# One-hot weight rows of the expert stage: one 256-column VectorE operation per token replaced by two of 128 columns

## The chip, the cores and the metric

The kernel runs on one core of one Trainium2 chip. The core has five engines with queues of their own: TensorE (PE; its weight loads are listed apart as PEld), VectorE (DVE), ScalarE (ACT), GpSimd (POOL) and SyncE (SP, which here only issues transfers). The metric is the device time of one execution in microseconds (us), as the median of several runs. Beside it there is one profiled execution with a trace of every instruction; its span runs from the first to the last instruction.

## What is computed

A transformer-like block (feed-forward, two kinds of attention, feed-forward) is followed by a second block with a long convolution, a gated recurrence and, at its end, a layer of 16,384 single-neuron experts. The change lies in that last layer, which the reference writes so:

```
s = jnp.einsum('blhpd,hpkd->blhpk', q, keys).astype(jnp.float32)
ts, ti = lax.top_k(s, K)
cand = ts[..., 0, :, None] + ts[..., 1, None, :]
cs, ci = lax.top_k(cand.reshape(B, L, PEER_HEADS, K * K), K)
e1 = jnp.take_along_axis(ti[..., 0, :], ci // K, axis=-1)
e2 = jnp.take_along_axis(ti[..., 1, :], ci % K, axis=-1)
experts = e1 * N_KEYS + e2
g = jax.nn.softmax(cs, axis=-1).astype(x.dtype)
...
act = jax.nn.gelu(jnp.einsum('td,tkd->tk', xt, u_tab[et])) * gt
return jnp.einsum('tk,tkd->td', act, v_tab[et])
```

There are 256 tokens. Each has 8 heads with 16 chosen experts, so 128 slots, and each slot has two indices (e1 and e2, both below 128) and a weight g.

## The kernel before

Nothing is gathered: the kernel works on all 16,384 experts for all tokens. Let an expert be the pair (e1, e2). A dense table of weights `gd` of shape [e1, e2, token] holds for each token its 128 weights at the chosen pairs and zero elsewhere. The products of the tokens with the first expert table (`us`) go through gelu to `st`, are multiplied by `gd` later, and then meet the second table (`vs`).

All large products are made in three TensorE passes over a high and a low part of each operand (`mm3`, L303 to L305). The weights come as tiles of 128 x 1024 numbers. A class `Stream` loads them on SP's queue (`raw`), lets ScalarE round them to the high part (`wh`, L247), and lets VectorE subtract to get the low part (`wl`, L249); it keeps four tiles ahead of TensorE.

In the stage of the change, from 1110 to 1387 us of the trace, TensorE runs down the first table. One call of `experts_in` (L1414) takes two table tiles of 128 experts; each tile is 8 x 3 matmuls of 256 columns. In between, a generator `weights_dense` (L1536) builds `gd` token by token; `paced` (L1575) calls it about three times for each table tile, so that it is through four tiles before the table ends. One step of the generator does this:

- for every fourth token, one VectorE operation (L1546) makes the one-hot rows of e1 of four tokens, 128 x 512 (tile `oh1`, printed as `oh`);
- for each token, VectorE makes the row of e2 (L1551, the changed line): per slot, 128 columns that hold the high part of g where the column is e2 and zero elsewhere, and 128 more with the low part. The tile is `oh2`, printed as `oh`; `iota` holds 0 to 127 in each partition, `eT` the indices and weights with the slots on partitions, `wp` the high and the low part of the weights;
- for the token four steps back (LAG), TensorE multiplies the two (L1561, 128 x 256 into PSUM), and for each pair of tokens ScalarE copies the low half to `gd` (L1566) and VectorE adds the high half (L1567).

The order on each engine is the order in which the program is written. VectorE's queue in this stage thus holds only four kinds of work: `wl` L249, the one-hot rows L1546 and L1551, and the sum L1567. The tile `oh2` has six buffers.

Of the kernel before, what the change touches and what calls it, by code (L numbers as in the profile page):

```python
# [10 lines left out]
F32 = mybir.dt.float32  # L11
# [5 lines left out]
ALU = mybir.AluOpType  # L17
# [265 lines left out]
def body(ctx, tc, a, o, upto=99):  # L283
    nc = tc.nc
# [6 lines left out]
    def psum(tag):  # L291
        return PS.tile([128, 512], F32, tag=tag, name=tag, bufs={"mm": 2, "acc": 3, "od": 1, "tr": 2}[tag])

    def accs():
        return [psum("acc"), psum("acc"), psum("acc"), psum("od")]
# [37 lines left out]
    def gemm_rows(acc, w, xh, xl, start, stop):  # L333
        h, lo = w
        for tt in range(2):
            ts_ = slice(tt * 128, tt * 128 + 128)
            for hf in range(2):
                cs = slice(hf * 512, hf * 512 + 512)
                mm3(acc[2 * tt + hf], xh[:, ts_], xl[:, ts_], h[:, cs], lo[:, cs], start, stop)

    def split(h, lo, src, eng=None):
        nc.scalar.copy(h, src)  # L342
        (eng or nc.vector).tensor_tensor(lo, src, h.bitcast(F32), op=ALU.subtract)  # L343
# [58 lines left out]
    def finish(acc, ops):  # L402

        for n, i in ((0, 0), (0, 1), (1, 0), (1, 1), (0, 2), (0, 3), (1, 2), (1, 3)):
            (h, lo), xh, xl = ops[n]
            ts_, cs = slice(i // 2 * 128, i // 2 * 128 + 128), slice(i % 2 * 512, i % 2 * 512 + 512)
            mm3(acc[i], xh[:, ts_], xl[:, ts_], h[:, cs], lo[:, cs], False, n == 1)
# [260 lines left out]
    with tc.tile_pool(name="mix", bufs=1) as MP:  # L668
# [300 lines left out]
        for b in range(4):  # L969
# [3 lines left out]
            for j in range(2):  # L973
# [4 lines left out]
                                           op0=ALU.add, op1=ALU.mult)  # L978
# [431 lines left out]
    iota = PP.tile([128, 128], F32, name="iota")  # L1410
    eT = [PP.tile([128, 3, 128], F32, name=f"eT{tt}") for tt in range(2)]
    stored = [DP.tile([128, 8 if i < 15 else 4, T], F32, name=f"act{i}") for i in range(16)]

    def experts_in(i, between=pump.step):  # L1414
        pt = psum("mm")
        gemm_w(pt[:, :T], ws.next(), xs_x)
        between()
        gemm_w(pt[:, T:], ws.next(), xs_x)
        st = PP.tile([128, 2, T], F32, tag="st", name="st", bufs=2)
        last[i] = st  # L1420
        nc.scalar.activation(st, pt.rearrange("p (e t) -> p e t", e=2), AF.Gelu_apprx_tanh)  # L1421
        if i < 62:
            nc.scalar.dma_start(stored[i // 4][:, 2 * (i % 4):2 * (i % 4) + 2, :], st)
# [107 lines left out]
    with tc.tile_pool(name="dense", bufs=1) as GP:  # L1531
        gd = GP.tile([128, 128, T], F32, name="gd")

        wp = GP.tile([128, 2, 128], F32R, name="wp")

        def weights_dense():  # L1536

            o1s, ohs = {}, {}
            for t in range(T + LAG):
                if t < T:  # L1540
                    tt, tl = divmod(t, 128)
                    if tl == 0:
                        split(wp[:, 0], wp[:, 1], eT[tt][:, 2])
                    if t % ONE == 0:
                        o1 = GP.tile([128, ONE, 128], F32R, tag="oh1", name="oh1", bufs=2)
                        nc.vector.tensor_tensor(o1, iota[:, None, :].to_broadcast([128, ONE, 128]),  # L1546
                                                eT[tt][:, 0, tl:tl + ONE, None].to_broadcast([128, ONE, 128]),
                                                op=ALU.is_equal)
                        o1s[t // ONE] = o1
                    oh = GP.tile([128, 2, 128], F32R, tag="ow", name="oh2", bufs=6)  # L1550
                    nc.vector.scalar_tensor_tensor(oh, iota[:, None, :].to_broadcast([128, 2, 128]),  # L1551
                                                   eT[tt][:, 1, tl:tl + 1],
                                                   wp[:, :, tl:tl + 1].bitcast(F32).to_broadcast([128, 2, 128]),
                                                   op0=ALU.is_equal, op1=ALU.mult)
                    ohs[t] = oh
                u = t - LAG
                if u >= 0:
                    if u % 2 == 0:
                        pt = psum("acc")
                    oh = ohs.pop(u)  # L1560
                    nc.tensor.matmul(pt[:, u % 2 * T:u % 2 * T + T], o1s[u // ONE][:, u % ONE],  # L1561
                                     oh.rearrange("p n e -> p (n e)"), start=True, stop=True)
                    if u % 2 == 1:
                        v = pt.rearrange("p (t n e) -> p n e t", t=2, n=2)
                        g = gd[:, :, u - 1:u + 1]
                        nc.scalar.copy(g, v[:, 1])  # L1566
                        nc.vector.tensor_tensor(g, v[:, 0], g, op=ALU.add)  # L1567
                yield

        pump.add(weights_dense())  # L1570
        left = 128 - 2 * n_in[0]
        total = T + LAG
        busy = left - 4

        def paced(i):  # L1575
            for _ in range(min(i + 1, busy) * total // busy - min(i, busy) * total // busy):
                pump.step()

        sv = {}

        def fetch(b):
            if b < 16:
                sv[b] = P0.tile([128, 8, T], F32, tag="lT" if b % 2 else "hT", name="sv")
                nc.gpsimd.dma_start(sv[b][:, :8 if b < 15 else 4, :], stored[b])

        order = list(range(124, 128)) + list(range(124))

        def act_split(n):
            e = order[n]
            src = last[e // 2] if e >= 124 else sv[e // 8][:, e % 8 - e % 2:e % 8 - e % 2 + 2, :]  # L1590
            if e % 2 == 0:
                nc.vector.tensor_tensor(src, src, gd[:, e:e + 2, :], op=ALU.mult)  # L1592
            ah = GP.tile([128, T], F32R, tag="ow", name="ah", bufs=6)
            al = GP.tile([128, T], F32R, tag="ow", name="al", bufs=6)
            split(ah, al, src[:, e % 2])
            if e % 8 == 7 and e < 120:
                fetch(e // 8 + 2)
            return ah, al

        for i in range(left // 2):  # L1600
            experts_in(n_in[0] + i, lambda: paced(2 * i))
            paced(2 * i + 1)
            if i == left // 2 - 2:
                pump.drain()
                ws.pool_every = 0
                nxt = [act_split(0), act_split(1)]
        fetch(0)
        fetch(1)
        acc = accs()
        for n in range(126):  # L1610
            nxt.append(act_split(n + 2))
            ah, al = nxt.pop(0)
            gemm_rows(acc, ws.next(), ah, al, n == 0, False)
        gf = P0.tile([128, D], F32, tag="raw", name="gf", bufs=RAW)
        nc.scalar.dma_start(gf, a["gains"][FINAL:FINAL + 1, :].to_broadcast([128, D]))
        x2 = [P0.tile([128, D], F32, tag="raw", name="x2", bufs=RAW) for tt in range(2)]
        for tt in range(2):
            nc.scalar.dma_start(x2[tt], res[tt * 128:(tt + 1) * 128, :])
        finish(acc, [(ws.next(), *nxt[n]) for n in range(2)])
        jk = P0.tile([128, 1024], F32, tag="wh", name="jk", bufs=NH)  # L1620
        ys = [P0.tile([128, D], F32, tag="wl", name="ys", bufs=NL) for tt in range(2)]
        rs = [None, None]

        def scaled(tt, hf):
            y = ys[tt][:, HALVES[hf]]
            if hf:
                nc.scalar.activation(y, y, AF.Copy, scale=rs[tt])
            else:
                nc.vector.tensor_scalar(y, y, rs[tt], None, op0=ALU.mult)
            (nc.scalar if tt and hf else nc.sync).dma_start(o[tt * 128:tt * 128 + 128, HALVES[hf]], y)  # L1630

        for tt in range(2):
            fn = RowNorm(GP, lambda hf: x2[tt][:, HALVES[hf]], jk[:, :512])
            for hf, sl in enumerate(HALVES):
                nc.vector.tensor_tensor(x2[tt][:, sl], acc[2 * tt + hf], x2[tt][:, sl], op=ALU.add)
                fn.half(hf)
            if tt:
                scaled(0, 0)
                scaled(0, 1)
            for sl in HALVES:  # L1640
                nc.vector.tensor_tensor(ys[tt][:, sl], x2[tt][:, sl], gf[:, sl], op=ALU.mult)
            rs[tt] = fn.root()
        for hf in range(2):
            scaled(1, hf)
# [19 lines left out]
```

## Time and profile before

| what | value |
|---|---|
| median of 3 runs | 1755.02 us |
| lowest, highest | 1753.38, 1756.79 us |
| the profiled execution | 1756.68 us |
| its span | 1754.9 us |
| PE busy over the span | 98% |
| DVE busy over the span | 74% |
| ACT busy over the span | 53% |

Busy shares over the whole span mix many stages. A matmul's record reaches over the start of the next one, and so does a VectorE operation's; the distance from start to start is what a queue of such operations costs.

### The profile page before, as it was taken

How to read it: one execution, taken by the hardware profiler on the slowest of the kernel's cores; microseconds unless marked ns; L12 is line 12 of the kernel's file. 1: busy time of each engine (PE TensorE's matmuls, PEld its weight loads, DVE VectorE, ACT ScalarE, POOL GpSimd, SP SyncE). 2: the span in 40 equal slices, each digit the busy share in tenths (PEclk: the TensorE clock that was granted, in tenths of full speed). 3: DMA queues.
4: the chain of work that ended last, by engine and by line, in shares of the span. 5: the costliest groups of instructions: out<-in, count | busy, mean ns of one | idle time of the engine just before them, and what ended most of it. 6: DMA issues, size and time to landing. Idle time of an engine off the chain costs nothing.

```text
span 1754.9 us, 30439 instructions
## 1 busy us (share of the span) xinstructions
PE 1719.0 (98%) x11794; PEld 1573.9 (90%) x11794; DVE 1307.4 (74%) x2237; ACT 931.7 (53%) x1524; POOL 151.3 (9%) x151
## 2 busy tenths in 40 slices
PE   8999999999999999999999999999999999999998
PEld 7999899999899987998899999999999988888886
DVE  5665678846765654788777999999999876766775
ACT  5544556654465444778444455555555544555544
POOL 3000100000100111000004634000000000000000
PEclk9999999999999999999899999999999999999999
DMA  7646464444466553453166567666665677776674
GB/s 231 201 160 201 144 192 145 135 154 134 145 215 199 187 164 129 158 192 121 60 193 204 175 223 225 217 193 198 195 199 190 216 253 236 255 243 239 238 246 166
DMA packets 93410, 332.08 MB, mean 189 GB/s; under 512 B 10552, under 2 KB 10707, under 8 KB 90960
## 3 DMA queue, kind: packets, MB, share of 16 engines
q1 hardware_dynamic: 79488, 287.73, 51.0%
q0 software_dynamic: 3696, 21.67, 3.5%
q10 hardware_dynamic: 10080, 20.71, 3.3%
q8 instruction: 93, 1.52, 0.4%
q14 instruction: 53, 0.43, 0.1%
HBM read 311.73 MB, written 18.35 MB: 188 GB/s over the span
## 4 chain that ended last, share of the span: by engine, by line
PE 79%; DVE 15%; issue 3%; ACT 1%; DMA 1%; POOL 1%; POOLq 0%; SPq 0%; ACTq 0%; DVEq 0%
PE mm L303 14%; PE mm L305 14%; PE mm L304 14%; PE acc L305 8%; PE acc L303 8%; PE acc L304 8%; DVE oh L1551 5%; DVE wl L249 3%; PE od L303 2%; PE od L304 2%; PE od L305 2%; DVE gd L1567 2%; DVE oh L1546 2%; PE tr L1305 1%; PE acc L719 1%
## 5 line engine op out<-in xcount | busy, mean ns | idle before, releaser
L249 DVE TENSOR_TENSOR wl<-raw,wh 128x1024 fp32r<-128x1024 f32 x508 | 620.9, 1226 | 281.5 <-ACT wh L247 279.7
L303 PE MATMUL mm<-hT,wh 128*128 128x256 f32 (+1 forms) x2496 | 711.4, 285 | 0.4 <-ACT qb L1462 0.4
L304 PE MATMUL mm<-lT,wh 128*128 128x256 f32 (+1 forms) x2496 | 703.3, 282 | 0.0
L305 PE MATMUL mm<-hT,wl 128*128 128x256 f32 (+1 forms) x2496 | 702.9, 282 | 0.0
L247 ACT CAST wh<-raw 128x1024 fp32r<-128x1024 f32 x544 | 570.2, 1052 | 181.3 <-PE mm L304 71.8
L303 PEld LDWEIGHTS mm<-hT,wh 128*128 128x128 f32 x2496 | 471.9, 189 | 8.3 <-issue 4.3
L304 PEld LDWEIGHTS mm<-lT,wh 128*128 128x128 f32 x2496 | 470.4, 188 | 3.4 <-issue 1.4
L305 PEld LDWEIGHTS mm<-hT,wl 128*128 128x128 f32 x2496 | 472.2, 189 | 0.0
L303 PE MATMUL acc<-wh,ah 128*128 128x512 f32 x516 | 202.0, 391 | 0.0
L305 PE MATMUL acc<-wh,al 128*128 128x512 f32 x516 | 201.8, 391 | 0.0
L304 PE MATMUL acc<-wl,ah 128*128 128x512 f32 x516 | 201.4, 390 | 0.0
L342 ACT CAST ah<-sv 128x256 fp32r<-128x256 f32 x124 | 50.5, 407 | 156.7 <-DVE sv L1592 126.6
L1551 DVE SCALAR_TENSOR_TENSOR oh<-iota,eT,wp 128x256 fp32r<-128x256 f32 x256 | 116.1, 483 | 0.0
L305 PEld LDWEIGHTS acc<-wh,al 128*128 128x128 f32 x516 | 96.9, 188 | 20.9
L304 PEld LDWEIGHTS acc<-wl,ah 128*128 128x128 f32 x516 | 97.0, 188 | 19.4 <-issue 0.2
L303 PEld LDWEIGHTS acc<-wh,ah 128*128 128x128 f32 x516 | 96.9, 188 | 19.4 <-issue 0.3
L249 POOL TENSOR_TENSOR wl<-raw,wh 128x1024 fp32r<-128x1024 f32 x36 | 86.1, 2406 | 58.4 <-ACT wh L247 58.4
L1421 ACT ACTIVATE st<-mm 128x512 f32<-128x512 f32 x64 | 38.4, 600 | 96.5 <-PE mm L305 96.2
L343 DVE TENSOR_TENSOR al<-sv,ah 128x256 fp32r<-128x256 f32 x124 | 52.5, 423 | 35.1 <-ACT ah L342 35.0
L1566 ACT COPY gd<-acc 128x256 f32<-128x256 f32 x128 | 46.6, 402 | 58.8 <-PE acc L1561 42.2
L303 PE MATMUL od<-wh,ah 128*128 128x512 f32 x172 | 67.3, 391 | 0.0
L304 PE MATMUL od<-wl,ah 128*128 128x512 f32 x172 | 67.2, 390 | 0.0
(390 smaller groups left out, 2053.6 us busy)
## 6 DMA issues: line engine op xcount, KB each, us to landing
raw<-in_ws_dram SPq DMA_DIRECT2D x288, 512.0 KB, 3.7
raw<-in_us_dram SPq DMA_DIRECT2D x128, 512.0 KB, 3.6
raw<-in_vs_dram SPq DMA_DIRECT2D x128, 512.0 KB, 4.2
act<-st ACTq DMA_DIRECT2D x62, 256.0 KB, 2.7
sv<-act POOLq DMA_DIRECT2D x15, 1024.0 KB, 7.2
gate_w<-in_gate_w_dram ACTq DMA_DIRECT2D x2, 1024.0 KB, 5.8
gain<-in_gains_dram POOLq DMA_DIRECT2D x3, 512.0 KB, 7.1
res<-x SPq DMA_DIRECT2D x2, 512.0 KB, 4.5
```

The lines of the kernel that those rows point to most:

```text
L247: nc.scalar.copy(h, raw)
L249: eng.tensor_tensor(lo, raw, h.bitcast(F32), op=ALU.subtract)
L303: nc.tensor.matmul(out, lh, rh, start=start, stop=False)
L304: nc.tensor.matmul(out, lh, rl, start=False, stop=False)
L305: nc.tensor.matmul(out, ll, rh, start=False, stop=stop)
L342: nc.scalar.copy(h, src)
L343: (eng or nc.vector).tensor_tensor(lo, src, h.bitcast(F32), op=ALU.subtract)
L1421: nc.scalar.activation(st, pt.rearrange("p (e t) -> p e t", e=2), AF.Gelu_apprx_tanh)
L1546: nc.vector.tensor_tensor(o1, iota[:, None, :].to_broadcast([128, ONE, 128]), eT[tt][:, 0, tl:tl + ONE, None].to_broadcast([128, ONE, 128] ...
L1551: nc.vector.scalar_tensor_tensor(oh, iota[:, None, :].to_broadcast([128, 2, 128]), eT[tt][:, 1, tl:tl + 1], wp[:, :, tl:tl + 1].bitcast(F3 ...
L1566: nc.scalar.copy(g, v[:, 1])
L1567: nc.vector.tensor_tensor(g, v[:, 0], g, op=ALU.add)
```

## The change

The changed line makes the row of one token. Before, one operation with two tensor inputs covered both halves: `iota`, read twice, is compared with the token's e2 (one number per partition, read from `eT`), and multiplied by a second tensor input, the two columns of `wp` spread over 128 columns each. After, each half is an operation of its own with one tensor input (`iota`) and two numbers per partition, e2 from `eT` and the weight from `wp`.

```diff
                     oh = GP.tile([128, 2, 128], F32R, tag="ow", name="oh2", bufs=6)
-                    nc.vector.scalar_tensor_tensor(oh, iota[:, None, :].to_broadcast([128, 2, 128]),
-                                                   eT[tt][:, 1, tl:tl + 1],
-                                                   wp[:, :, tl:tl + 1].bitcast(F32).to_broadcast([128, 2, 128]),
-                                                   op0=ALU.is_equal, op1=ALU.mult)
+                    for j in range(2):
+                        nc.vector.tensor_scalar(oh[:, j], iota, eT[tt][:, 1, tl:tl + 1],
+                                                wp[:, j, tl:tl + 1].bitcast(F32), op0=ALU.is_equal, op1=ALU.mult)
```

On VectorE, in the middle of the stage, stood these rows for parts of three table tiles (`oh` with a 128x512 shape is the one-hot of four tokens, with 128x256 the changed row):

```order
L1546 TENSOR_TENSOR oh_13658<-iota,eT_9964 128x512
L1551 SCALAR_TENSOR_TENSOR oh_13660<-iota,eT_9964,wp 128x256
L1551 SCALAR_TENSOR_TENSOR oh_13664<-iota,eT_9964,wp 128x256
L1567 TENSOR_TENSOR gd<-acc,gd 128x128x2
L1551 SCALAR_TENSOR_TENSOR oh_13669<-iota,eT_9964,wp 128x256
L249 TENSOR_TENSOR wl<-raw,wh 128x1024
```

At the same place there stand now:

```order
L1546 TENSOR_TENSOR oh_13750<-iota,eT_9964 128x512
L1552 TENSOR_SCALAR oh_13752<-iota,eT_9964,wp 128x128 x2
L1552 TENSOR_SCALAR oh_13757<-iota,eT_9964,wp 128x128 x2
L1566 TENSOR_TENSOR gd<-acc,gd 128x128x2
L1552 TENSOR_SCALAR oh_13763<-iota,eT_9964,wp 128x128 x2
L249 TENSOR_TENSOR wl<-raw,wh 128x1024
```

Each of the 256 rows of L1551 has become two, in the same place, and nothing else has moved; the lines behind the change count one less. On TensorE, ScalarE, GpSimd and SyncE no row differs but for these line numbers.

## Rows read from the trace of the kernel before

**Rows 1.** The page's part 1, busy time of the engines.

```profile
PE 1719.0 (98%) x11794; PEld 1573.9 (90%) x11794; DVE 1307.4 (74%) x2237; ACT 931.7 (53%) x1524; POOL 151.3 (9%) x151
```

**Rows 2.** Windows: length, busy us of PE, PEld, DVE, ACT, POOL; PEclk; DMA.

```profile
1110.00:1200.00 90.00, 88.69 (x738) 87.44 (x737) 90.00 (x172) 47.85 (x82) 0.00 (x0) 1.00 0.62 199
1200.00:1300.00 100.00, 97.56 (x804) 95.58 (x803) 99.99 (x194) 53.08 (x91) 0.00 (x0) 1.00 0.61 194
1300.00:1387.00 87.00, 85.24 (x705) 83.78 (x704) 87.00 (x167) 46.28 (x80) 0.00 (x0) 1.00 0.61 197
1387.00:1400.00 13.00, 13.00 (x106) 12.68 (x104) 8.76 (x11) 6.85 (x12) 1.09 (x2) 1.00 0.65 208
1400.00:1755.00 355.00, 346.51 (x1529) 286.69 (x1527) 243.53 (x323) 174.47 (x261) 10.46 (x20) 1.00 0.69 236
```

**Rows 3.** Waits of TensorE, 1110 to 1387 us: total, times, longest.

```profile
PE acc L1561 <- DVE oh L1551: 3.5, 13, 0.5
```

**Rows 4.** Groups of instructions by line, 1110 to 1387 us: busy us, mean ns.

```profile
L303 PE MATMUL mm<-hT,wh 128*128 128x256 f32 x662 | 185.5, 280 | 0.0
...
L1551 DVE SCALAR_TENSOR_TENSOR oh<-iota,eT,wp 128x256 fp32r<-128x256 f32 x256 | 116.1, 483 | 0.0
L249 DVE TENSOR_TENSOR wl<-raw,wh 128x1024 fp32r<-128x1024 f32 x83 | 101.3, 1221 | 0.0
L1567 DVE TENSOR_TENSOR gd<-acc,gd 128x256 f32<-128x256 f32 x126 | 55.5, 440 | 0.0
...
L1546 DVE TENSOR_TENSOR oh<-iota,eT 128x512 fp32r<-128x512 f32 x64 | 43.9, 687 | 0.0
```

**Rows 5.** Timeline of VectorE in the middle of the stage: start us, us.

```profile
1182.08 1.21 DVE L249 TENSOR_TENSOR wl<-raw,wh 128x1024 fp32r<-128x1024 f32 x1
1183.21 0.68 DVE L1546 TENSOR_TENSOR oh<-iota,eT 128x512 fp32r<-128x512 f32 x1
1183.81 0.87 DVE L1551 SCALAR_TENSOR_TENSOR oh<-iota,eT,wp 128x256 fp32r<-128x256 f32 x2
1184.61 0.43 DVE L1567 TENSOR_TENSOR gd<-acc,gd 128x256 f32<-128x256 f32 x1
1184.96 0.47 DVE L1551 SCALAR_TENSOR_TENSOR oh<-iota,eT,wp 128x256 fp32r<-128x256 f32 x1
1185.35 1.21 DVE L249 TENSOR_TENSOR wl<-raw,wh 128x1024 fp32r<-128x1024 f32 x1
```

**Rows 6.** Timeline of TensorE: first and last of ten matmuls in a row.

```profile
1138.82 0.28 PE L305 MATMUL mm<-hT,wl 128*128 128x256 f32 x1
...
1139.88 0.28 PE L305 MATMUL mm<-hT,wl 128*128 128x256 f32 x1
```

**Rows 7.** VectorE groups over the whole span, shapes apart: busy us, mean ns.

```profile
L499 DVE SCALAR_TENSOR_TENSOR lT<-tr,col_t,hT 128x256 fp32r<-128x256 f32 x20 | 8.7, 478 | 5.2 <-ACT hT L498 5.2
...
L1279 DVE TENSOR_SCALAR hu<-hyp,col_t 128x272 f32<-128x272 f32 x12 | 4.9, 412 | 0.0
L353 DVE SCALAR_TENSOR_TENSOR lT<-mg,hT 128x256 fp32r<-128x256 f32 x8 | 3.4, 420 | 0.5 <-ACT hT L352 0.5
...
L559 DVE TENSOR_SCALAR rr_k<-rr_k 128x256 f32<-128x256 f32 x2 | 0.6, 294 | 0.1
...
L1494 DVE TENSOR_SCALAR pos<-pos 128x128 f32<-128x128 f32 x2 | 0.5, 228 | 0.1
...
L640 DVE TENSOR_SCALAR ropeS<-ropeS,col_t 128x256 f32<-128x256 f32 x1 | 0.3, 348 | 0.0
```

**Rows 8.** Timeline of VectorE, two stretches with operations that wait for nothing.

```profile
57.01 0.29 DVE L566 TENSOR_SCALAR ropeC<-ropeC 128x256 f32<-128x256 f32 x1
57.22 0.35 DVE L640 TENSOR_SCALAR ropeS<-ropeS,col_t 128x256 f32<-128x256 f32 x1
...
480.17 0.48 DVE L452 TENSOR_SCALAR xn<-x,rstd 128x512 f32<-128x512 f32 x1 [0.73 <-POOL rstd L425]
480.58 0.48 DVE L456 TENSOR_SCALAR xn<-x,rstd 128x512 f32<-128x512 f32 x1
```

## The prediction

> **What bounds the kernel now.** The page's busy times come first: TensorE is busy for 98% of the span and VectorE for 74% [rows 1], which reads like a kernel that TensorE bounds and in which VectorE's work is free. Busy shares are means over stages, so I looked next at the stage of the change alone, in windows [rows 2]. From 1110 to 1387 us VectorE is busy for the whole of every window (90.00 of 90, 99.99 of 100, 87.00 of 87). Right behind it, from 1387 to 1400 us, it is busy for 8.76 of 13 us, and in the last 355 us for 243.53. TensorE is busy for almost all of the stage too, so busy time alone doesn't say which of the two sets the pace.
>
> Counts do. The groups of the stage [rows 4] give 662 matmuls on L303 (L304 and L305 have 662 each as well) and 256 on L1561, one per token: 2242. Ten in a row start 1.06 us apart from first to last, so one costs 0.118 us [rows 6]. TensorE's own work is 2242 x 0.118 = 264.6 us of 277, so it stands still for about 12.4 us. For VectorE I take distances from start to start in the timeline [rows 5]: 1.13 us from a `wl` to the next operation, 0.60 from L1546, 0.35 from L1567, and 0.80 for two and 0.39 for one of L1551, so 0.397 each. With the counts of [rows 4]: 83 x 1.13 + 64 x 0.60 + 126 x 0.35 + 256 x 0.397 = 93.8 + 38.4 + 44.1 + 101.6 = 277.9 us, which is the stage's length. VectorE works back to back and sets the pace here, and the matmuls of L1561 are seen to wait for the row of L1551 [rows 3]. A nanosecond more or less per token on VectorE is thus 0.256 us of the kernel, with one limit: less than 12.4 us can be gained before TensorE takes over. A loss has no limit. Nothing behind the stage gives it back, since there TensorE is the busier engine (13.00 of 13, 346.51 of 355) [rows 2].
>
> **What the change removes and adds.** It removes 256 operations of 0.397 us. It adds 512 of 128 columns with one tensor input and two numbers per partition, and the trace of before has none of just that form. I build its price from the same kind of operation with other columns and scalars.
>
> *Columns.* L1494 (128 columns, no number read per partition) takes 228 ns, L559 (256 columns, the same) 294 ns [rows 7]: 66 ns for 128 columns, 0.52 ns each. The old operation has two tensor inputs, and such operations go at about 1.04 ns: L353 takes 420 ns for its 256 columns, `wl` with 1024 columns 1221 ns [rows 4, 7], so 801 ns for 768. The columns of the pair therefore cost 2 x 66 = 132 ns where the old ones cost about 267. That is what the new form saves, some 135 ns per token.
>
> *Fixed part and scalars.* With no per-partition number, 256 columns take 294 ns; with one, L640 takes 348, so 54 more [rows 7]. L1279 reads two (`hy_w` and `hy_b`) for 272 columns and takes 412 ns. Its columns are 272 x 0.52 = 141, which leaves 271 ns, against 348 - 133 = 215 with one number and 294 - 133 = 161 with none. Each number read per partition costs about 55 ns. The same step is there for the old form: 420 ns for L353, whose scalar is a constant, and 478 for L499, whose scalar is read [rows 7].
>
> The new operation should thus last 271 + 66 = 337 ns. What the queue pays is less, since the next operation starts before the last has ended: 0.29 us of length against 0.21 from start to start at 57.01 us, 0.48 against 0.41 at 480.17 us [rows 8], and 483 ns against 397 for L1551 itself [rows 4, 5]. With 85 ns of overlap the price is 252 ns. A second way goes by starts alone: 210 - 133 = 77 ns of fixed part without a number, 410 - 267 = 143 with one [rows 8], so about 200 with two, and 266 with the columns; those rows have a grain of 10 ns. I take 256, nearer to the first, which has the more exact means. The pair costs 512 ns.
>
> The Trainium skill has a lower fixed part ("VectorE: DVE Perf Modes", The TRN2 errata): an operation from memory to memory takes 58 cycles at 0.96 GHz and one more per column, or per two columns in the doubled mode. By my estimate from that page the pair takes 254 ns and the old operation 327, so VectorE would have 18.7 us less to do instead of 29.4 more. The trace disagrees: the old operation pays 397 ns, and an operation with one read scalar 143 beside its columns [rows 5, 8].
>
> *Sum.* 512 - 397 = 115 ns per token, by 256 tokens 29.4 us more on VectorE, all of it on the path. The stage grows from 277 to about 306 us, and TensorE stands still for 41.8 instead of 12.4 us of it, in the same place: at L1561, for its row. What is late next: behind the pair on VectorE stand the sum of L1567 and the next `wl`, so ScalarE's copies and the following table tile come later by as much, but they wait behind the same queue and add nothing.
>
> *What costs nothing.* TensorE, ScalarE and the transfers get no new instruction. GpSimd has none in the stage (x0) [rows 2], so a delay from that side isn't to be had. The second operation of a pair writes the other half of its tile and reads nothing that the first wrote, so I give it no wait.
>
> *Bounds of the unknown price.* From below: the second operation's scalars might be read under the first one's columns, so that the pair costs what two operations with one number do, 2 x (143 + 66) = 418 ns by starts or 2 x (215 + 66 - 85) = 392 by lengths; that is +21 to -5 ns per token, +5.4 to -1.3 us. From above: if a one-input operation that writes `fp32r` goes at the slow column rate (every row above of one input writes `f32`), an operation costs 271 + 133 - 85 = 319 ns, the pair 638, and the kernel 61.7 us more. Nearest to the new form is L1279, with the same operation and as many scalars, and by it the price stands.
>
> **The rivals.**
>
> 1. *The reads of the scalars hide.* As worked out, the pair costs 392 to 418 ns, and the time stays at 1754 to 1760 us. For it: consecutive operations do overlap by 85 ns [rows 5, 8]. Against it: the step per scalar shows from start to start as well (77 and 143 ns), so one read is not hidden.
>
> 2. *Faster: the fixed part shrinks in a row of like operations.* Both halves read the same `iota` and the same e2, and if a pair then paid only the 77 ns of an operation without scalars, it would cost 2 x (77 + 66) = 286 ns, 111 less than now. VectorE would need 277 - 28.4 = 248.6 us, TensorE becomes the bound at 264.6, and the gain is its 12.4 us: 1755.0 - 12.4 = 1742.6. The change is a gain as soon as the fixed part falls below 397 / 2 - 66 = 132 ns. The rows with one scalar stand at 143 already, so this has little behind it. The Trainium skill's formula above comes out here as well ("VectorE: DVE Perf Modes", The TRN2 errata): its pair is 73 ns cheaper than its old operation.
>
> 3. *The slow column rate for `fp32r`.* 1755.0 + 61.7 = 1816.7 us. For it: no row shows a one-input operation of VectorE that writes `fp32r`. Against it: both types have four bytes, and with two inputs the type makes no difference (L1567 writes `f32` and has 440 ns, L353 `fp32r` and 420) [rows 4, 7].
>
> 4. *The clock falls.* TensorE would stand still for 14% of the stage instead of 4%. Its granted clock is 1.00 in all windows here [rows 2]; if it sank to 0.5 now and then, an unlucky stretch of 10 us would cost up to 5 us more, some 1790 to 1800 in all. VectorE's pace hides most of that.
>
> **How the numbers follow.** The profiled execution took 1756.7 us, and the median of the three runs is 1755.0; the sum carries over to either: 1786.1 and 1784.4. I give the forecast (slower by 20 to 37 us) 78%, rival 1 7%, rival 2 4%, rival 3 7%, rival 4 4%. The forecast's own bounds are a price of 238 to 270 ns per operation, a choice that reaches somewhat beyond the two ways above (252 and 266); the time is 1775 to 1792. The range of 1768 to 1797 adds half of the way to rival 1 and most of rival 4, and leaves the other three out. A measurement here can tell about 0.2%, or 3.5 us, from no change: slower 0.89, same 0.07 (the larger part of rival 1), faster 0.04.
>
> **What would show it right or wrong.** In the profile after, the 512 new operations should last about 337 ns and start about 256 ns apart; 290 or less would speak for rivals 1 and 2, 400 for rival 3. VectorE should still be busy in the whole stage, which should end near 1416 us, with `wl`, L1546 and the sums unchanged, and the waits of L1561 for its row should grow by about 29 us. The stages before 1110 us and after it should keep their lengths. I am wrong if the pair overlaps more than rows with other neighbours do, or if TensorE's clock sinks.

## The result, and the profile after

The changed kernel takes 1786.64 us (median of 4, 1784.6 to 1789.12) against 1754.37 us in the same set of runs. The ratio estimated from the single runs is 1.0171, with a 95% interval of 1.0155 to 1.0186; the two medians by themselves give 1.0184. That is slower by 27 to 33 us; 29.4 was forecast. The profiled execution took 1784.6 us with a span of 1782.7.

The page's part 1 after the change, to be read beside [rows 1]:

```profile
span 1782.7 us, 30694 instructions
PE 1726.1 (97%) x11792; PEld 1573.9 (88%) x11794; DVE 1337.3 (75%) x2493; ACT 933.0 (52%) x1524; POOL 151.2 (8%) x151
```

VectorE has 256 instructions more (2493 against 2237) and 29.9 us more of busy time. No other engine has more instructions. The windows of the stage, in the columns of [rows 2] (length, busy us and instructions of PE, PEld, DVE, ACT and POOL, clock, DMA):

```profile
1110.00:1200.00 90.00, 82.81 (x663) 79.43 (x662) 90.00 (x229) 43.82 (x74) 0.00 (x0) 1.00 0.54 179
1200.00:1300.00 100.00, 91.43 (x724) 86.97 (x723) 100.00 (x256) 48.81 (x84) 0.00 (x0) 1.00 0.54 177
1300.00:1415.00 115.00, 105.08 (x835) 100.29 (x834) 115.00 (x296) 56.28 (x94) 0.00 (x0) 1.00 0.54 175
1415.00:1430.00 15.00, 15.00 (x114) 14.36 (x114) 9.85 (x14) 8.41 (x14) 1.08 (x2) 1.00 0.66 220
```

From 1200 to 1300 us VectorE now passes 256 instructions instead of 194, while TensorE passes 724 matmuls instead of 804: the same 100 us hold a tenth less of TensorE's work. The clock stays at 1.00, and the matmuls that run without a pause still start 0.118 us apart.

The timeline of VectorE (start us, us) gives the price directly:

```profile
1183.03 0.71 DVE L1546 TENSOR_TENSOR oh<-iota,eT 128x512 fp32r<-128x512 f32 x1
1183.63 0.62 DVE L1552 TENSOR_SCALAR oh<-iota,eT,wp 128x128 fp32r<-128x128 f32 x2
1184.14 1.25 DVE L249 TENSOR_TENSOR wl<-raw,wh 128x1024 fp32r<-128x1024 f32 x1
1185.28 0.62 DVE L1552 TENSOR_SCALAR oh<-iota,eT,wp 128x128 fp32r<-128x128 f32 x2
...
1186.14 1.13 DVE L1552 TENSOR_SCALAR oh<-iota,eT,wp 128x128 fp32r<-128x128 f32 x4
1187.17 0.46 DVE L1566 TENSOR_TENSOR gd<-acc,gd 128x256 f32<-128x256 f32 x1
```

From 1183.63 to 1184.14 us two operations pass, from 1186.14 to 1187.17 four: 0.51 and 1.03 us, 256 ns each. The other operations keep their prices: 0.60 us for L1546, 1.14 for `wl`, where [rows 5] gave 0.60 and 1.13. The stage can be measured from its first operation to the `wl` behind the last row of a token. Before, that is 276.8 us:

```profile
1110.01 0.68 DVE L1546 TENSOR_TENSOR oh<-iota,eT 128x512 fp32r<-128x512 f32 x1
...
1386.79 1.24 DVE L249 TENSOR_TENSOR wl<-raw,wh 128x1024 fp32r<-128x1024 f32 x1
```

and after:

```profile
1107.21 0.68 DVE L1546 TENSOR_TENSOR oh<-iota,eT 128x512 fp32r<-128x512 f32 x1
...
1414.61 1.55 DVE L249 TENSOR_TENSOR wl<-raw,wh 128x1024 fp32r<-128x1024 f32 x1
```

307.4 us, so 30.6 more. In this one execution the stages ahead were 2.8 us shorter, which is why its total grew by 27.9 only; the medians grew by 32.3.

### The profile page after: what moved, and what is told of

It reads as the page before. It is cut to its first block, busy times and chain, and to the rows that moved or that the text cites. A ratio compares the mean times of both kernels' runs of the same rounds, so it can differ in the third digit from the quotient of the medians.

```text
span 1782.7 us, 30694 instructions
## 1 busy us (share of the span) xinstructions
PE 1726.1 (97%) x11792; PEld 1573.9 (88%) x11794; DVE 1337.3 (75%) x2493; ACT 933.0 (52%) x1524; POOL 151.2 (8%) x151
## 4 chain that ended last, share of the span: by engine, by line
PE 76%; DVE 18%; issue 3%; ACT 1%; DMA 1%; POOL 1%; POOLq 0%; SPq 0%; ACTq 0%; DVEq 0%
PE mm L303 13%; PE mm L305 13%; PE mm L304 13%; PE acc L305 7%; DVE oh L1552 7%; PE acc L303 7%; PE acc L304 7%; DVE wl L249 3%; DVE gd L1566 3%; PE od L303 2%; PE od L304 2%; PE od L305 2%; DVE oh L1546 2%; PE tr L1305 1%; PE acc L719 1%
## 5 line engine op out<-in xcount | busy, mean ns | idle before, releaser
L249 DVE TENSOR_TENSOR wl<-raw,wh 128x1024 fp32r<-128x1024 f32 x508 | 627.7, 1239 | 283.9 <-ACT wh L247 282.4
L1552 DVE TENSOR_SCALAR oh<-iota,eT,wp 128x128 fp32r<-128x128 f32 x512 | 159.8, 424 | 0.0
L1560 PE MATMUL acc<-oh,oh 128*128 128x256 f32 x256 | 62.2, 309 | 26.2 <-DVE oh L1552 21.0
L1560 PEld LDWEIGHTS acc<-oh,oh 128*128 128x128 f32 x256 | 42.1, 188 | 39.2 <-ACT st L1421 14.1
```

What stands on the lines that cost most here:

```text
L249: eng.tensor_tensor(lo, raw, h.bitcast(F32), op=ALU.subtract)
L1552: nc.vector.tensor_scalar(oh[:, j], iota, eT[tt][:, 1, tl:tl + 1], wp[:, j, tl:tl + 1].bitcast(F32), op0=ALU.is_equal, op1=ALU.mult)
```

## The experiments

**Half of the tokens.** Is the loss spread evenly over the operations, or does something tip over?

```diff
-                    for j in range(2):
+                    if t % 2:
+                        for j in range(2):
                             nc.vector.tensor_scalar(oh[:, j], ...)
+                    else:
+                        nc.vector.scalar_tensor_tensor(oh, ...)
```

> Every second token is made by the pair, the others by the old operation. If VectorE's queue sets the pace and the pair costs 512 ns against 397, half of 29.4 us is lost: 14.7 us over the kernel before, about 1769. If the loss came from one place or one threshold (a buffer that runs dry, a clock that falls), it would be nearly 0 or nearly all of the 32 us.

Measured: 1773.01 us against 1757.12 of the kernel before, 1.0098 (1.0077 to 1.0119). Half of the tokens cost 15.9 us, about half of the loss; nothing tips over.

**One scalar read, and none.** What in the new operation costs that much? The two runs replace one or both of the numbers read per partition by constants.

```diff
-nc.vector.tensor_scalar(oh[:, j], iota, eT[tt][:, 1, tl:tl + 1], wp[:, j, tl:tl + 1].bitcast(F32), ...)
+nc.vector.tensor_scalar(oh[:, j], iota, eT[tt][:, 1, tl:tl + 1], 0.5, ...)      # one read
+nc.vector.tensor_scalar(oh[:, j], iota, 5.0, 0.5, ...)                          # no read
```

> The pair multiplies by the constant 0.5 in place of the weight read from memory, so the weights are left out of the result; e2 is still read. If each read scalar costs about 57 ns, an operation starts 200 ns after the last, a pair takes 400, and the time comes out at that of the kernel before, 1755 (+-3). If a VectorE operation costs a flat sum whatever it reads, the time stays at 1786.

> The pair compares with the constant 5 and multiplies by 0.5, so it reads no scalar, and the result leaves out indices and weights of this row. By the price per read scalar an operation starts 143 ns after the last and a pair takes 286; VectorE needs 249 us in the stage, TensorE with its 264.6 becomes the bound, and the time is 12.4 us under the kernel before, about 1742. With a flat sum per operation it stays at 1786. If TensorE were not next behind VectorE, the gain would go on to 28 us.

Measured: 1755.61 us with one read (0.9992, 0.9981 to 1.0003), 1746.05 with none (0.9944, 0.9923 to 0.9965), both against 1757.12. The timeline of VectorE with one read:

```profile
1200.62 0.87 DVE L1552 TENSOR_SCALAR oh<-iota,eT 128x128 fp32r<-128x128 f32 x4
1201.40 0.47 DVE L1566 TENSOR_TENSOR gd<-acc,gd 128x256 f32<-128x256 f32 x1
```

and with none:

```profile
1203.51 0.63 DVE L1552 TENSOR_SCALAR oh<-iota 128x128 fp32r<-128x128 f32 x4
1204.05 0.43 DVE L1566 TENSOR_TENSOR gd<-acc,gd 128x256 f32<-128x256 f32 x1
```

Four operations take 0.78 us with one read and 0.54 without, so 195 and 135 ns each, beside 256 with two. Each scalar that an operation reads from memory costs 60 ns, and the rest of it 135. The second read scalar thus decides: two operations with one read cost just what the old one does (2 x 195 = 390 against 397), and the time is the same. The run without reads shows what stands behind VectorE, in its windows:

```profile
1200.00:1300.00 100.00, 100.00 (x846) 100.00 (x846) 94.92 (x301) 55.49 (x97) 0.00 (x0) 1.00 0.68 204
```

TensorE is now busy for 100.00 of 100 us with 846 matmuls, and VectorE has pauses. The pairs now save 256 x (397 - 270) ns = 32.5 us of VectorE's work, but the kernel gains 11.

**Without the sum.** Is the pair dear for VectorE's queue only, or does TensorE also lose by waiting for two writers of a tile? Both kernels run without VectorE's sum of the halves, which gives VectorE's queue room:

```diff
                         nc.scalar.copy(g, v[:, 1])
-                        nc.vector.tensor_tensor(g, v[:, 0], g, op=ALU.add)
```

> The changed kernel without VectorE's sum of the two halves (L1566), so only the low half of the weights gets into the table. VectorE has 126 x 0.35 = 44.1 us less in the stage: 306.5 - 44.1 = 262.4 us, just under TensorE's 264.6. If the loss is only VectorE's queue, it is gone: 1742 to 1748. If the pair costs TensorE something by itself (two writers of a tile to wait for), about 30 us of loss stay over the same cut of the kernel before.

> The kernel before without VectorE's sum of the two halves, the same cut as in the run of the changed kernel without the sum. VectorE needs 277 - 44.1 = 233 us in the stage, TensorE 264.6, so TensorE sets the pace: 12.4 us under the kernel before, about 1742. By the theory of VectorE's queue the two cut kernels lie within 6 us of each other, with the rival they are 30 us apart.

Measured: the new kernel without the sum 1744.06 us (0.9931, 0.9905 to 0.9956, against 1757.12), the old one 1745.91 (0.9944, 0.9924 to 0.9963, against 1757.30). Each is compared with the kernel before in its own set of runs, and the two intervals overlap. With room in VectorE's queue the change costs nothing that can be measured here, where some 6 us would show. The window of the new kernel without the sum:

```profile
1200.00:1300.00 100.00, 100.00 (x845) 99.95 (x845) 99.60 (x250) 55.86 (x96) 0.00 (x0) 1.00 0.66 206
```

VectorE is still busy almost throughout, but TensorE passes 845 matmuls, as many as without any read. The two engines are about even here, as 262.4 against 264.6 us said.

**TensorE adds the halves.** A version of the whole computation without the sum on VectorE, once with the old operation and once with the pair:

```diff
-                    nc.tensor.matmul(pt[:, u % 2 * T:u % 2 * T + T], o1s[u // ONE][:, u % ONE],
-                                     oh.rearrange("p n e -> p (n e)"), start=True, stop=True)
+                    for j in range(2):
+                        nc.tensor.matmul(pt[:, u % 2 * 128:u % 2 * 128 + 128], o1s[u // ONE][:, u % ONE], oh[:, j],
+                                         start=j == 0, stop=j == 1)
                     if u % 2 == 1:
-                        v = pt.rearrange("p (t n e) -> p n e t", t=2, n=2)
-                        g = gd[:, :, u - 1:u + 1]
-                        nc.scalar.copy(g, v[:, 1])
-                        nc.vector.tensor_tensor(g, v[:, 0], g, op=ALU.add)
+                        v = pt[:, :256].rearrange("p (t e) -> p e t", t=2)
+                        nc.scalar.copy(gd[:, :, u - 1:u + 1], v)
```

> The kernel before, but TensorE adds the two halves itself: two matmuls of 128 columns into the same 128 columns of PSUM instead of one of 256, one copy by ScalarE, no sum on VectorE. The whole computation is done. VectorE needs 233 us. TensorE has 256 matmuls more: if one of 128 columns costs half of 0.118 us, it needs about 265 us and the kernel takes about 1742; if it costs 0.118 as well, 294.8 us and 1772.

> The same with the pair of the changed kernel. VectorE needs 262.4 us. The time should be that of the run with the old operation and TensorE's own addition, or up to 5 us more where both engines are about even (1742 to 1748, or 1772 with the dear matmul).

Measured: 1770.99 us with the old operation (1.0089, 1.0066 to 1.0113), 1771.78 with the pair (1.0085, 1.0062 to 1.0108), against 1757.30. So it is the dear matmul, and again old and new operation make no difference, now under TensorE's bound. The timeline of TensorE in the run with the old operation shows the price:

```profile
1201.37 0.78 PE L1562 MATMUL acc<-oh,oh 128*128 128x128 f32 x6
1201.98 0.34 PE L303 MATMUL mm<-hT,wh 128*128 128x256 f32 x1
1202.16 0.28 PE L304 MATMUL mm<-lT,wh 128*128 128x256 f32 x1
```

Six matmuls of 128 columns take 0.61 us, 0.10 each, and the next step is 0.18 instead of 0.12 us. Each of them has a weight load of its own (the trace has 510 loads for 511 such matmuls), though the two of a token use the same weights. In this form half the columns save next to nothing.

**The even point.** Each sum that leaves VectorE saves 0.35 us there and costs TensorE two matmuls. Before the change VectorE was ahead by 12.4 us, so a part of the sums can go: every sixth pair of tokens takes the form above, the others the old one (`both = u // 2 % 6 == 5`).

> The whole computation, with the old row operation; for every sixth pair of tokens TensorE adds the two halves itself. VectorE has 21 sums of 0.35 us less, 269.6 us; TensorE 42 matmuls of about 0.115 us more, 269.5. If both engines only count their own work, the gain is about 7 us: 1750 against 1757, 0.4%. If the two queues disturb each other where they are even, it is less, down to nothing.

Measured: 1751.74 us (11 runs) against 1757.22 (16 runs), 0.9967 (0.9956 to 0.9978). This version, with the old row operation and the whole computation, beats the kernel before by 5.5 us, where 7 were expected, and the changed kernel by more. Its window:

```profile
1200.00:1300.00 100.00, 99.52 (x842) 99.26 (x841) 99.90 (x189) 55.00 (x96) 0.00 (x0) 1.00 0.63 202
```

Both engines are busy nearly throughout, at 99.52 and 99.90 of 100 us.

**ScalarE weights the rows.** ScalarE is busy for half of the stage. In two runs it takes the weights over for every fourth or every second token, so that VectorE's operation has one tensor input of 128 columns and one read:

```diff
+                    if t % 4 == 3:      # second run: t % 2
+                        nc.vector.tensor_scalar(oh[:, 1], iota, eT[tt][:, 1, tl:tl + 1], None, op0=ALU.is_equal)
+                        for j in range(2):
+                            nc.scalar.activation(oh[:, j], oh[:, 1].bitcast(F32), AF.Copy,
+                                                 scale=wp[:, j, tl:tl + 1].bitcast(F32))
+                    else:
                         nc.vector.scalar_tensor_tensor(oh, ...)
```

> The whole computation; for every fourth token VectorE only makes the 0/1 row of 128 columns with one read scalar (196 ns in the run with one read), and ScalarE multiplies it by the high and by the low weight. VectorE has 64 x (397 - 196) ns = 12.9 us less in the stage, 264.1 us, about TensorE's 264.6. If only VectorE's queue holds the stage, the kernel takes 1744 to 1749 against 1757 of the kernel before in these runs, some 0.5 to 0.7% less. If ScalarE's products come too late behind its own rounding and copies, TensorE waits for them and little or nothing is gained.

> The same for every second token: 25.7 us less for VectorE, 251 us, and 256 more operations for ScalarE, which has about half of the stage free. TensorE sets the pace: 1744 to 1746, or no better than the run with every fourth token if the products on ScalarE come late.

Measured: 1831.82 us (1.0441, 1.0426 to 1.0456) and 1921.18 (1.0939, 1.0925 to 1.0953), against 1757.22. The gains that both expectations led with were far off, and on the wrong side: both runs lose, and the run with every second token is "no better", as its second branch allowed, by far more than it said. The waits of the run with every fourth token, 1120 to 1400 us (us in total, times, longest):

```profile
ACT oh L1555 <- DVE oh L1553: 124.7, 50, 3.3
DVE gd L1573 <- ACT gd L1572: 59.0, 50, 1.2
PE acc L1567 <- DVE oh L1557: 50.7, 53, 1.5
...
DVE wl L249 <- ACT wh L247: 7.8, 16, 0.5
```

and its timeline, VectorE and then ScalarE:

```profile
1204.25 0.28 DVE L1553 TENSOR_SCALAR oh<-iota,eT 128x128 fp32r<-128x128 f32 x1
1205.71 0.43 DVE L1573 TENSOR_TENSOR gd<-acc,gd 128x256 f32<-128x256 f32 x1 [1.18 <-ACT gd L1572]
```

```profile
1204.57 0.84 ACT L1555 ACTIVATE oh<-oh,wp 128x128 fp32r<-128x128 f32 x2 [3.03 <-DVE oh L1553]
1205.31 0.65 ACT L1572 COPY gd<-acc 128x256 f32<-128x256 f32 x2
```

The other engines run ahead of VectorE here. So ScalarE stands at its products until VectorE has made the row, and the copy that VectorE needs next stands behind those products. VectorE then waits 1.18 us, about once for each such token: 73.2 us in 62 waits over the whole stage of this run, 1107 to 1462 us. The waits for the rounded weights add 10.9 us there. Less the 12.9 us of work saved, that is 71.2 us; the run lost 74.6.

**The same, two tokens later.** The two products come after the copies of the next steps (at the step t + 2; at token 127 of a block at once, since `wp` is then written anew).

> As the run in which ScalarE weights every fourth token, but ScalarE's two products come two tokens later in its queue. If the 75 us lost there were VectorE's wait of 1.18 us for a copy that stood behind those products (64 times), the wait goes, VectorE needs 264.1 us in the stage and TensorE 264.6: 1744 to 1750 against 1757. If ScalarE's products are dear by themselves (their length, or the reads of the weights), the time stays above 1800.

> The same for every second token. If the late place removes the wait, VectorE needs 251 us, ScalarE has about 80 us more to do in a stage of which it has half free, and TensorE sets the pace: 1743 to 1748. If ScalarE's queue becomes tight, TensorE waits for rows and the time lies above the run with every fourth token.

Measured: 1790.56 us (1.0206, 1.0180 to 1.0232) and 1849.74 (1.0537, 1.0515 to 1.0560), against 1756.93. The later place took away more than half of the loss at every fourth token, but the gain that both expectations led with did not come: the first run lies between its two branches, and the second lies above the first, as its second branch said. The waits at every fourth token, 1120 to 1400 us:

```profile
ACT gd L1569 <- PE acc L1564: 44.4, 45, 3.3
...
PEld acc L1564 <- ACT oh L1574: 33.2, 19, 2.2
PE acc L1564 <- ACT oh L1574: 27.3, 18, 2.0
...
DVE gd L1570 <- ACT gd L1569: 18.7, 30, 1.6
```

Now the products stand behind copies that wait for TensorE, and TensorE waits for the products. VectorE waits as well, 18.7 us for the copies and 18.8 for the rounded weights. With four steps between a row and its matmul, neither of the two places tried in ScalarE's queue is free of such waits. Whether more steps would do, or a separate order of the copies, wasn't tried. In the two runs with every second token the granted clock was 0.91 and 0.92 as a mean from 1120 to 1400 us, with TensorE busy for 211 and 228 of these 280 us; what part of their loss is the clock's wasn't separated.

## Why the prediction was right

**The bound.** VectorE's queue set the pace of the stage, though TensorE was busy for 98% of the span: right. Half the tokens lose half the time; with room in VectorE's queue, old and new take the same time, within what these runs can tell.

**The limit of a gain.** TensorE's 12.4 us behind it: right. Without reads the gain was 11.1 us and without the sum 11.4 to 13.1, though up to 44 us of VectorE's work were gone.

**The price of the pair.** 256 ns from start to start: measured 256. With one read the prediction's starts give 143 + 66 = 209 ns and with none 77 + 66 = 143 (the expectation of the run with one read had 200): measured 195 and 135. The ladder from other shapes held within 14 ns, and the value lay between the two ways to get at it (252 and 266). That it was hit to the nanosecond is luck, since 256 was a choice between the two.

**The doubled column rate** holds for outputs of `fp32r` as well. With L1494's 66 ns of columns, 135 ns leave 69 of fixed part; at the slow rate the columns alone would take 133. Rival 3 falls.

**Rivals 1 and 2.** Neither reads nor fixed parts hide in a row of like operations: two neighbours with the same `iota` and the same e2 still start 256 ns apart. By the Trainium skill's formula ("VectorE: DVE Perf Modes", The TRN2 errata) the pair would have been cheaper than the old operation. That doesn't hold here, with 512 ns against 397. An estimate from that page for one operation of 128 columns is 58 + 64 cycles at 0.96 GHz, 127 ns; the trace has 135 without a scalar, which is near, and 256 with two. What the formula lacks is the reads. Rival 4: the clock stayed at 1.00 in the stage.

**What was off.** The stage grew by 30.6 us, 1.2 more than the forecast's 29.4, whose prices were read from a timeline with a grain of 10 ns. Added up from start to start over the whole stage, the 512 new operations take 131.1 us and the 256 old ones 101.2 (395 ns each, not 397), which is 29.8 more; the sums of L1566 take 44.9 against 44.1, 0.8 more. `wl` and L1546 are the same within 0.1.

Two of the prediction's signs by length pointed the wrong way. The operation was forecast to last 337 ns, and 400 would speak for rival 3; the median is 402. By the lengths the operations also overlap by 146 ns instead of 85, and more overlap was to show the forecast wrong. Only the starts, 256 ns apart, say that neither matters. Where the ends don't drift (last section) both terms hold: in the changed kernel without the sum the median is 343 ns, so 87 of overlap.

The wait of L1560 for its row was to grow by 29 us; its own line, from 1107 to 1415 us, grew from 3.5 [rows 3] to 21.0:

```profile
PE acc L1560 <- DVE oh L1552: 21.0, 37, 1.0
PEld acc L1560 <- ACT st L1421: 14.1, 18, 1.1
PEld acc L1560 <- ACT gd L1565: 10.7, 13, 1.2
PEld acc L1560 <- issue: 7.2, 13, 0.6
PEld acc L1560 <- DVE oh L1552: 6.6, 25, 0.3
```

The rest of the pauses at the same matmuls is listed as waits of the weight load, most of it under the name of ScalarE. ScalarE has no more work than before, and none of these waits is left in the changed kernel without the sum, so the name is probably that of an event that came late for the same reason. The starts are clearer than the names: the steps into and out of the matmuls of L1560 exceed 118 ns by 44.8 us in all, against 12.2 before the change, and all other steps of the stage by less than 1 us either way. About 1 us of the growth comes from records that are missing. So TensorE's new pauses, some 32 us, lie where the prediction put them.

## What to carry to other kernels

Take the time of a queue from start to start in the stage, not from busy shares or from the lengths of the records. A VectorE operation here is a sum of a fixed part, its columns and its scalars read from memory (69, 66 and 60 ns each for 128 columns), and splitting an operation in two pays only if the doubled column rate saves more than a second fixed part and the reads that are added. Here it saves 135 ns and adds 69 + 3 x 60 = 249. By the same parts the old operation, with one read and 267 ns of columns, should cost 396 ns, and it costs 395 to 397. An engine that is idle for half of a stage was in these runs no place for work between two in-order queues, since neither spot tried in its queue was free of waits for them.

## What the hardware showed that was not expected

With two scalars read, VectorE's operations kept starting 256 ns apart, but ended later and later. The view of the tile, over all 512 (shortest, median, longest in ns):

```profile
L1552 DVE TENSOR_SCALAR oh<-iota,eT,wp x512: 331/402/690, 1107.8 to 1414.0; 128x128 fp32r<-128x128 f32 x171
```

and the timeline near the end of the stage:

```profile
1410.74 0.94 DVE L1552 TENSOR_SCALAR oh<-iota,eT,wp 128x128 fp32r<-128x128 f32 x2
1411.25 1.56 DVE L249 TENSOR_TENSOR wl<-raw,wh 128x1024 fp32r<-128x1024 f32 x1
```

A pair that took 0.62 us at 1183.63 takes 0.94 at 1410.74, and the `wl` behind it 1.56 instead of 1.25, while the `wl` still starts 0.51 us after the pair. So up to three operations are under way at once in the records. The late end cost no pace: the starts stayed 256 ns apart. In the run with one read the lengths stay together:

```profile
L1552 DVE TENSOR_SCALAR oh<-iota,eT x512: 258/269/290, 1110.5 to 1385.3; 128x128 fp32r<-128x128 f32 x171
```

They also stay together with two reads in the two runs where VectorE has pauses, the changed kernel without the sum and the pair with TensorE's addition:

```profile
L1552 DVE TENSOR_SCALAR oh<-iota,eT,wp x512: 329/343/368, 1109.6 to 1373.0; 128x128 fp32r<-128x128 f32 x171
```

```profile
L1552 DVE TENSOR_SCALAR oh<-iota,eT,wp x512: 339/347/381, 1112.3 to 1400.7; 128x128 fp32r<-128x128 f32 x171
```

So two reads alone don't make the ends drift. They drift in the changed kernel and in the run with half of the tokens (337/454/645 ns), where the operations with two reads stand in a queue without pauses. The two runs without drift also lack VectorE's sum, so it isn't shown which of the two keeps the ends in place.

The other surprise is TensorE's: a matmul of 128 columns with a weight load of its own costs 0.10 to 0.11 us in a row of six, against 0.118 for one of 256, which has one too.
